# A decoder layer on one core: one grouped product in place of three in the compressed branch, and eight empty steps placed elsewhere

## The chip, the cores and the metric

The kernel runs on one core of a Trainium2 chip. The core has five engines with a queue each: TensorE (PE, and PEld for its weight loads), VectorE (DVE), ScalarE (ACT), GpSimd (POOL) and SyncE (SP, which issues most DMAs). The metric is device time in microseconds (us) of one execution. A measurement is the median of several runs, and one more execution is taken with the hardware profiler.

## The reference, cut to what matters

One layer of a decoder with 256 tokens of width 2048, all in float32. After an RMS norm and one input projection, two groups of heads run side by side: gated linear attention (GLA, 4 heads) and sparse attention (NSA, 8 query heads in 2 groups that share keys and values). Their outputs go into one output projection, then a SwiGLU feed-forward part (FFN) follows.

NSA has three branches: compressed, selected and sliding window. The compressed one is what the change touches:

```python
k_cmp = rms_norm(compress(heads(kc_raw, hk), k_pos, k_w1, k_w2), kc_g)
v_cmp = compress(heads(vc_raw, hk), v_pos, v_w1, v_w2)        # silu(flat @ w1) @ w2
...
sc = jnp.einsum('bhgqd,bhnd->bhgqn', qb, k_cmp) * scale
pc = jax.nn.softmax(jnp.where(mc, sc, NEG), axis=-1) * mc
o_cmp = jnp.einsum('bhgqn,bhnd->bhgqd', pc, v_cmp)
...
return gb[..., 0:1] * o_cmp + gb[..., 1:2] * o_sel + gb[..., 2:3] * o_win
```

There are only 15 compressed keys and values per head (`NCMP = 15`).

## The kernel before

**Three products for one.** The matrix products read float32 in a faster, less exact form (`F32R`). To keep the precision, a number is split into a high part, which is what that form can hold, and a low part, the rest. A product then becomes three: high times high, high times low, low times high. `split` (L131) does this for the weights: ACT writes `hi` (L137), DVE subtracts and writes `lo` (L138). `in_parts` (L637) does it for activations with ACT (L638) and DVE (L639). `chunk` (L273) issues the main stream of products (L283): 24 of 128x512 for every four tiles of 128 rows of weights, and each `hi`/`lo` pair of buffers serves 12 of them. Four such buffers of each exist.

**Main stream and side steps.** Most of the kernel before the FFN is written as generators. `drive` (L98) walks through the main generator (`proj` or `w_out_half`) and counts two units per product or pair of products; whenever the count reaches `pace`, `side` (L83) lets one side generator take one step, up to its next `yield`. `urgent` goes ahead of `later`. An empty step (a bare `yield`) takes the turn and issues nothing, so it lets the main stream run on by that much. The pace is 2.5 units (a step for each 1.25 products) while the projections of keys, values and queries run, and 2 (a step for each product) in `w_out_half(0)`, the first half of the output projection, which has 192 main products.

The generators in question, in their order in `later`:

- `gla_mix` (L644): `gla_decay(0)` makes the decay factors for two GLA heads on ACT and DVE, level by level (L542 to L564); after 4 empty steps `gla_scores` (L567) begins with its products (L581), which read them; `gla_out` (L599) follows one head behind.
- `compress` (L736): blocks of raw keys and values times `w1` (L766, weights by DMA from POOL's queue at L745), a SiLU (L778), then `w2` (L783 for keys, L799 for values). The values' result, 15 rows per head group, is split into `vcm[0]` (high) and `vcm[1]` (low). Both tiles have 128 rows and are zero below row 15.
- `nsa_mix` (L917): for each of four tiles (group kv, token half t) `nsa_scores` (L836), and one tile behind it `nsa_out` (L883). `nsa_scores` ends with the softmax of the compressed scores `c` (L863 to L874) and the scaling of the other probabilities (L880). In `nsa_out`, `turn(i)` transposes probabilities on PE (L210) and splits them; `turn(0)` is that of `c`. The products with the values (L913) then add up in one bank of PSUM: three for each `i`, with a step each.

`turn_q` (L825), an urgent one, waits 11 empty steps after a query projection, then transposes the queries (L210) that DVE has copied out of PSUM (L814). `sum_rows` (L1035) is a third kind: in the background it adds rows of FFN weights on DVE (L1046) and stores the sums by two DMAs from POOL's queue (L1050).

The framework that builds the program decides each engine's final order: text order is the priority, but an instruction that it expects to be ready late lets later ones pass. So the trace, not the text, tells where an instruction stands. Tiles named `g` come from pools of rotating buffers (`g4` 24, `g2` 13, `g1` 7).

Of the kernel before, what the change touches and what calls it, by code (L numbers as in the profile page):

```python
# [9 lines left out]
F32R = mybir.dt.float32r  # L10
BF16 = mybir.dt.bfloat16
AF = mybir.ActivationFunctionType
ALU = mybir.AluOpType
AX = mybir.AxisListType

P = 128
S = 256
# [9 lines left out]
NCMP = 15  # L27
# [10 lines left out]
def kernel(  # L38
# [4 lines left out]
    nc = tc.nc  # L43
    act, mm = nc.scalar.activation, nc.tensor.matmul
    TT, TS, STT = nc.vector.tensor_tensor, nc.vector.tensor_scalar, nc.vector.scalar_tensor_tensor
# [7 lines left out]
    cp = tc.alloc_tile_pool(name="cp", bufs=1)  # L53
# [5 lines left out]
    def slot(pool, tag, bufs, align=None):  # L59
        def f(shape, dt=F32):  # L60
            n_tiles[0] += 1
            return pool.tile([P] + list(shape), dt, tag=tag, bufs=bufs, name=f"{tag}_{n_tiles[0]}", align_bytes=align)
        return f
# [3 lines left out]
    g4, g2, g1, small = slot(gp, "g4", 24, LINE), slot(s2p, "g2", 13), slot(s1p, "g1", 7), slot(s1p, "sm", 12)  # L67

    def bank():
        n_tiles[0] += 1  # L70
        return pp.tile([P, 512], F32, tag="bank", name=f"bank_{n_tiles[0]}")
# [5 lines left out]
    def f32(t):  # L77
        return t.bitcast(F32)
# [94 lines left out]
    cw2 = cp.tile([P, 2, P], F32, name="cw2")  # L173
# [35 lines left out]
    def transpose(o, i, n=P):  # L209
        return nc.tensor.transpose(o, i, ident[:n, :n])  # L210
# [426 lines left out]
    def in_parts(hi, lo, ps):  # L637
        act(hi, ps, AF.Copy)  # L638
        last["d"] = TT(lo, ps, f32(hi), ALU.subtract)  # L639
# [4 lines left out]
    def gla_mix():  # L644
        res = [{} for _ in range(4)]
        yield from gla_decay(0)
        for _ in range(4):
            yield
        nxt = iter(())
        for h in range(4):  # L650
            if h == 1:
                nxt = gla_decay(1)
            if h == 2:
                yield from nxt
            for _ in gla_scores(h, res[h]):
                yield
                next(nxt, None)
            if h:
                yield from gla_out(h - 1, res[h - 1])
        for _ in range(7):  # L660
            yield
        yield from gla_out(3, res[3])


    st = {}
# [62 lines left out]

    kcm = cp.tile([P, 2 * NCMP], F32, name="kcm")

    vcm = [cp.tile([P, 2, P], F32R, name=f"vcm{i}") for i in range(2)]
    for v in vcm:
        nc.gpsimd.memset(f32(v), 0.0)
    N2 = 2 * NCMP

    def compress():  # L736

        uT = st["uT"]

        def rows_of(i):  # L740

            res = []
            for j in range(2):
                to, j0 = g4([8, P]), (i % 2 * 2 + j) * 1024
                nc.gpsimd.dma_start(to, (k_w1, v_w1)[i // 2][0, j0:j0 + 1024, :].rearrange("(j p) h -> p j h", p=P))  # L745
                res.append(to)
            return res

        nxt = rows_of(0)
        for w in range(2):  # L750
            ph = bank()
            nc.vector.memset(ph[:, :P], 0.0)
            for half in range(2):
                j0 = 16 * half
                r = nxt
                if 2 * w + half < 3:
                    nxt = rows_of(2 * w + half + 1)
                blk = g2([16, 2, NCMP])
                for h in range(2):
                    u = uT[:, w, h, j0:j0 + 240].rearrange("p (n j) -> p j n", j=16)  # L760
                    TT(blk[:, :, h, :], u, pos[:, w, j0:j0 + 16].unsqueeze(2).to_broadcast([P, 16, NCMP]), ALU.add)
                for _ in range(9):
                    yield
                for j in range(16):
                    g = 32 * (j % 4)
                    mm(ph[g:g + N2, :P], blk[:, j].rearrange("p h n -> p (h n)"), r[j // 8][:, j % 8, :], start=(half == 0 and j < 4),  # L766
                       stop=(half == 1 and j >= 12), tile_position=(0, g), skip_group_check=True)
                    if j % 16 == 15:
                        yield
            hs = g1([P])  # L770
            nc.vector.tensor_copy(hs, ph[:, :P])
            for _ in range(6):
                yield
            pt = bank()
            transpose(pt[:, :P], hs)
            hid = g1([32])
            nc.vector.tensor_reduce(hid, pt[:, :P].rearrange("p (g m) -> p m g", g=4), AX.X, ALU.add)
            act(hid, hid, AF.Silu)  # L778
            for _ in range(9):
                yield  # L780
            pk = bank()
            if w == 0:
                mm(pk[:N2, :P], hid[:, :N2], cw2[:, 0, :], start=True, stop=True)  # L783
                ss = small([1])
                junk = g1([P])
                act(junk[:N2], pk[:N2, :P], AF.Square, accum_out=ss[:N2])
                TS(ss[:N2], ss[:N2], 1.0 / 128, EPS, ALU.mult, ALU.add)
                rk = small([1])
                rsqrt_(rk[:N2], ss[:N2])
                kk = g1([P])  # L790
                TS(kk[:N2], pk[:N2, :P], rk[:N2], None, ALU.mult)
                for _ in range(25):
                    yield
                pt = bank()
                transpose(pt[:, :N2], kk[:N2, :], N2)
                TS(kcm, pt[:, :N2], kgain[:, 0:1], None, ALU.mult)
            else:
                for h in range(2):
                    mm(pk[:NCMP, h * P:(h + 1) * P], hid[:, h * NCMP:(h + 1) * NCMP], cw2[:, 1, :], start=True, stop=True)  # L799
                in_parts(vcm[0][:NCMP], vcm[1][:NCMP], pk[:NCMP, :S].rearrange("p (h d) -> p h d", h=2))  # L800
            yield

    nq, sc = {}, {}
# [19 lines left out]
        return f  # L823

    def turn_q(kv, q):  # L825
        for _ in range(11):
            yield
        qf, qh, ql = g4([4, S]), g4([4, S], F32R), g4([4, S], F32R)
        for pair in range(2):
            js = slice(2 * pair, 2 * pair + 2)  # L830
            ps = yield from turn_pair(q, pair)
            in_parts(qh[:, js], ql[:, js], ps)
            nc.scalar.copy(qf[:, js], ps)
        nq[kv] = qf, qh, ql

    def nsa_scores(kv, t, res):  # L836
# [5 lines left out]
        pr = [g4([2, 2, ns]) for _ in range(2)] if t else [g4([4, 2, ns])]  # L842
        pr = [pr[j // 2][:, j % 2] if t else pr[0][:, j] for j in range(4)]
        mxs, nb, sums = small([4, 2]), small([4, 2]), small([4, 2])
        pc_ = bank()
        for j in range(4):
            p = bank()
            sv = p[:, :2 * ns].rearrange("p (b s) -> p b s", b=2)
            for i, (a, b) in enumerate(((qh, kh), (qh, kl), (ql, kh))):
# [4 lines left out]
               start=True, stop=True)  # L854
# [7 lines left out]
        c = small([4, NCMP])  # L862
# [6 lines left out]
        sm = small([4])  # L869
# [1 line left out]
        nc.vector.reciprocal(sm, sm)  # L871
        TT(sm, sm, gv[:, 0, :], ALU.mult)
        TT(c, c, mone[:, t, :].unsqueeze(1).to_broadcast([P, 4, NCMP]), ALU.mult)
        TT(c, c, sm.unsqueeze(2).to_broadcast([P, 4, NCMP]), ALU.mult)  # L874
        rs = small([4, 2])
        nc.vector.reciprocal(rs, sums)
        TT(rs, rs, gv[:, 1:3, :].rearrange("p b h -> p h b"), ALU.mult)
        for j in range(4):
            for b in range(2):
                TS(pr[j][:, b, :], pr[j][:, b, :], rs[:, j, b:b + 1], None, ALU.mult)  # L880
        res.update(pr=pr, c=c)

    def nsa_out(kv, t, res):  # L883
        pr, c, tb = res["pr"], res["c"], slice(t * P, (t + 1) * P)
        if t == 0:
            m_h[2 + kv], m_l[2 + kv] = g4([4, S], F32R), g4([4, S], F32R)
        todo = [None] + [(b, s_) for b in range(2) for s_ in range(t + 1)]
        pts = []

        def turn(i):  # L890
            pt = bank()
            n = P if i else NCMP
            parts = [g2([512], F32R) for _ in range(2)]
            if i == 0:
                for a in parts:
                    nc.gpsimd.memset(f32(a), 0.0)
            for j in range(4):
                src = pr[j][:, todo[i][0], todo[i][1] * P:(todo[i][1] + 1) * P] if i else c[:, j, :]
                transpose(pt[:n, j * P:(j + 1) * P], src)
                if j % 2:  # L900
                    yield
            pts.append(parts)
            in_parts(parts[0][:n], parts[1][:n], pt[:n, :])

        po = bank()
        yield from turn(0)
        yield from turn(1)
        for i, at in enumerate(todo):
            if i + 2 < len(todo):
                yield from turn(i + 2)  # L910
            vh, vl = (st[v][:, at[0], at[1], kv * P:(kv + 1) * P] for v in ("vh", "vl")) if i else (v[:, kv, :] for v in vcm)
            for j, (v, p) in enumerate(((vh, pts[i][0]), (vh, pts[i][1]), (vl, pts[i][0]))):
                mm(po, v, p, start=(i == 0 and j == 0), stop=(i == len(todo) - 1 and j == 2))  # L913
                yield
        put_mix(2 + kv, slice(0, 4), tb, po.rearrange("p (j s) -> p j s", j=4))

# [460 lines left out]
```

## Time and profile before

| what | value |
|---|---|
| time, median of 3 runs | 1110.05 us (1109.75 to 1110.84) |
| time of the profiled execution | 1109.58 us |
| its span, first to last instruction | 1107.9 us |
| TensorE clock granted | 1.000 throughout |
| bytes moved | 259.61 MB, mean 234 GB/s |

The profiled execution is 1.7 us longer than its span, which is what lies around the instructions. A profile lists busy time per engine, a picture of the span in 40 slices of 27.7 us, the chain of work that ended last, and groups of instructions. Further views show single instructions in order of time (start in us, duration in us, engine, line, what it writes and reads, shapes, count; in brackets the idle time of the engine and what ended it), windows of time with the busy time of each engine, and who waited for whom. A busy PE is not a PE at its peak, because products overlap: what one costs in a stream is the distance from start to start. In time, the span goes: loading and the first projections to about 84 us, projections with GLA beside them to about 260, NSA beside the last projection and the first half of the output projection to about 370, the second half to about 418, the FFN to the end.

### The profile page before, as it was taken

To read this page: it belongs to the slowest core of one execution; us is meant where nothing else is said; L and a number is where in the kernel's file an instruction comes from. 1 tells how busy PE (TensorE), PEld (TensorE's weight loads), DVE (VectorE), ACT (ScalarE), POOL (GpSimd) and SP (SyncE) were. 2 spreads that over 40 slices of the span, in tenths; PEclk is the share of its full clock that TensorE was granted. 3 is DMA by queue.
4 is the path that set the end of the run, shared out by engine and by line. 5 is a ranking of instruction groups with operands and counts; after the bars stand their busy time and mean duration, and the time that the engine had idled before them with its cause. 6 is when DMAs were issued, how large, how long until landed. Compare 5 with 4: busy or idle time off the path is not lost.

```text
span 1107.9 us, 14624 instructions
## 1 busy us (share of the span) xinstructions
PE 1097.7 (99%) x5298; PEld 900.7 (81%) x5298; DVE 991.5 (89%) x1277; ACT 741.5 (67%) x1009; POOL 74.0 (7%) x139
## 2 busy tenths in 40 slices
PE   9999999999999999999999999999999999999998
PEld 8888887897777887888888888888888888887886
DVE  6678779987589788997999999999999999999997
ACT  7645557555566586667586866768586866767684
POOL 4110000123101000000000000000000000000000
PEclk9999999999999999999999999999999999999999
DMA  7999985568846656785565657576566657476663
GB/s 272 336 337 361 368 285 187 188 227 286 282 183 225 218 185 215 244 305 202 192 223 198 217 197 251 187 248 212 206 228 213 213 197 255 167 267 220 234 229 114
DMA packets 124850, 259.61 MB, mean 234 GB/s; under 512 B 6709, under 2 KB 8793, under 8 KB 124778
## 3 DMA queue, kind: packets, MB, share of 16 engines
q1 hardware_dynamic: 113514, 219.86, 57.3%
q0 software_dynamic: 10368, 37.75, 9.2%
q10 hardware_dynamic: 896, 1.07, 0.3%
q8 instruction: 41, 0.67, 0.2%
q14 instruction: 31, 0.25, 0.1%
HBM read 239.78 MB, written 18.87 MB: 233 GB/s over the span
## 4 chain that ended last, share of the span: by engine, by line
PE 83%; DVE 6%; DMA 6%; issue 2%; ACT 2%; SPq 0%; POOL 0%; ACTq 0%; POOLq 0%; DVEq 0%
PE bank L283 39%; PE bank L1114 35%; DMA raw<-in_w_in_dram 3%; PE bank L210 3%; DMA g<-in_w_up_dram 2%; PE bank L1255 2%; DVE ftwo L639 2%; DVE lo L138 2%; PE bank L913 1%; PE bank L850 1%; ACT hi L137 1%; PE bank L581 1%; DMA fraw<-in_w_down_dram 1%; DVE g L1145 0%; DVE g L1046 0%
## 5 line engine op out<-in xcount | busy, mean ns | idle before, releaser
L1114 PE MATMUL bank<-ftwo,g 128*128 128x512 f32 x1848 | 431.6, 392 | 0.2 <-ACT ftwo L638 0.2
L1114 PEld LDWEIGHTS bank<-ftwo,g 128*128 128x128 f32 x1848 | 342.4, 188 | 76.6 <-DVE ftwo L639 3.5
L283 PE MATMUL bank<-hi,g 128*128 128x512 f32 (+1 forms) x1088 | 321.7, 375 | 1.3 <-ACT hi L323 1.3
L639 DVE TENSOR_TENSOR ftwo<-fraw,ftwo 128x1536 fp32r<-128x1536 f32 (+1 forms) x130 | 257.6, 1982 | 9.0 <-ACT ftwo L638 7.6
L638 ACT ACTIVATE ftwo<-fraw 128x1536 fp32r<-128x1536 f32 (+1 forms) x130 | 217.0, 1671 | 32.7 <-DMA fraw<-in_w_up_dram 13.8
L283 PE MATMUL bank<-ftwo,g 128*128 128x512 f32 x960 | 221.4, 391 | 1.0 <-ACT bank L1226 1.0
L283 PEld LDWEIGHTS bank<-hi,g 128*128 128x128 f32 x1088 | 192.4, 188 | 31.4 <-ACT hi L323 1.7
L283 PEld LDWEIGHTS bank<-ftwo,g 128*128 128x128 f32 x960 | 179.2, 188 | 40.5 <-ACT bank L1226 3.1
L283 PE MATMUL bank<-lo,g 128*128 128x512 f32 (+3 forms) x544 | 194.5, 377 | 0.0
L137 ACT ACTIVATE hi<-raw 128x1024 fp32r<-128x1024 f32 (+3 forms) x124 | 130.7, 1057 | 90.5 <-PE bank L283 74.3
L138 DVE TENSOR_TENSOR lo<-raw,hi 128x1024 fp32r<-128x1024 f32 (+3 forms) x124 | 150.1, 1217 | 38.0 <-ACT hi L137 37.3
L638 ACT ACTIVATE ftwo<-g 128x1024 fp32r<-128x1024 f32 x74 | 78.2, 1057 | 69.0 <-DVE g L1145 43.7
L283 PEld LDWEIGHTS bank<-lo,g 128*128 128x128 f32 x544 | 98.6, 189 | 15.9 <-issue 0.8
L639 DVE TENSOR_TENSOR ftwo<-g,ftwo 128x1024 fp32r<-128x1024 f32 x74 | 90.2, 1219 | 10.7 <-ACT ftwo L638 10.7
L639 DVE TENSOR_TENSOR ftwo<-fsum,ftwo 128x1024 fp32r<-128x1024 f32 x74 | 90.1, 1217 | 0.0
L638 ACT ACTIVATE ftwo<-fsum 128x1024 fp32r<-128x1024 f32 x74 | 77.5, 1048 | 8.6 <-DVE fsum L1147 7.4
L1238 ACT COPY g<-bank 128x512 f32<-128x512 f32 x80 | 45.9, 589 | 39.7 <-PE bank L283 37.8
L1145 DVE TENSOR_TENSOR g<-fraw 128x1024 f32<-128x1024 f32 x56 | 67.4, 1217 | 0.0
L1226 ACT COPY bank<-g 128x512 f32<-128x512 f32 x80 | 45.2, 592 | 13.1 <-DVE f L1175 11.5
L638 ACT ACTIVATE g<-bank 128x512 fp32r<-128x512 f32 (+1 forms) x50 | 29.2, 592 | 36.2 <-PE bank L210 29.0
L1103 POOL DMA_DIRECT2D g<-sums x16 | 8.5, 533 | 512.1 <-DVE ftwo L639 482.3
L210 PE MATMUL bank<-ident,g 128*128 128x128 f32 (+2 forms) x214 | 40.1, 278 | 1.2 <-DVE g L814 0.5
(241 smaller groups left out, 902.2 us busy)
## 6 DMA issues: line engine op xcount, KB each, us to landing
fraw<-in_w_gate_dram SPq DMA_DIRECT2D x86, 512.0 KB, 3.8
fraw<-in_w_down_dram SPq DMA_DIRECT2D x42, 1024.0 KB, 5.0
raw<-in_w_in_dram SPq DMA_DIRECT2D x36, 1024.0 KB, 7.5
fraw<-in_w_up_dram SPq DMA_DIRECT2D x70, 512.0 KB, 4.6
sums<-g POOLq DMA_DIRECT2D x32, 512.0 KB, 6.5
raw<-in_w_out_dram SPq DMA_DIRECT2D x16, 1024.0 KB, 5.3
g<-in_w_gate_dram SPq DMA_DIRECT2D x16, 512.0 KB, 8.4
g<-in_w_up_dram SPq DMA_DIRECT2D x16, 512.0 KB, 8.6
```

Source lines behind the costliest of these rows:

```text
L137: act(h[:, i:i + n], r[:, k + i:k + i + n], AF.Copy)
L138: last["d"] = TT(o[:, i:i + n], r[:, k + i:k + i + n], f32(h[:, i:i + n]), ALU.subtract)
L210: return nc.tensor.transpose(o, i, ident[:n, :n])
L283: last["mm"] = mm(bk[t], a[:, k, t * P:(t + 1) * P], m[:, off:off + w], start=(first_ and k == 0 and i == 0), stop=(end and k == 3 and i = ...
L581: mm(p[:, j * P:(j + 1) * P], u, w, start=True, stop=True)
L638: act(hi, ps, AF.Copy)
L639: last["d"] = TT(lo, ps, f32(hi), ALU.subtract)
L1114: mm(banks[q], x, m, start=todo[q] == total[q], stop=todo[q] == 1)
L1145: TT(s1, r[:, 1:3], r[:, 3:4].to_broadcast([P, 2, 512]), ALU.add)
L1226: nc.scalar.copy(banks[qs[n][t]], h_sb[n][:, t, :])
L1238: nc.scalar.copy(h_sb[n][:, t, :], bs[t])
L1255: mm(bk, u, m, start=(first and i == 0), stop=(end and i == 2), skip_group_check=onto)
```

## The change

Three groups of 15 rows, each starting at a multiple of 32 (rows 0, 32 and 64, 79 rows in all), hold probabilities high, low, high and values high, high, low. One product over these rows adds up what three products gave.

```diff
     def gla_mix():
         yield from gla_decay(0)
-        for _ in range(4):
+        for _ in range(9):
             yield
...
-    vcm = [cp.tile([P, 2, P], F32R, name=f"vcm{i}") for i in range(2)]
-    for v in vcm:
-        nc.gpsimd.memset(f32(v), 0.0)
+    vcm = cp.tile([P, 2, P], F32R, name="vcm")
+    G3, N3 = 32, 2 * 32 + NCMP
+    def thrice(a):
+        return a.unsqueeze(2).to_broadcast([P, a.shape[1], 3, NCMP])
+    def groups(a):
+        return a[:, :, :3 * G3].rearrange("p h (g n) -> p h g n", n=G3)[:, :, :, :NCMP]
...
-            act(hid, hid, AF.Silu)
+            if w == 0:
+                act(hid, hid, AF.Silu)
+            else:
+                hid3 = g2([2, P])
+                nc.gpsimd.memset(hid3, 0.0)
+                act(groups(hid3), thrice(hid[:, :N2].rearrange("p (h n) -> p h n", h=2)), AF.Silu)
...
-                    mm(pk[:NCMP, h * P:(h + 1) * P], hid[:, h * NCMP:(h + 1) * NCMP], cw2[:, 1, :], start=True, stop=True)
-                in_parts(vcm[0][:NCMP], vcm[1][:NCMP], pk[:NCMP, :S].rearrange("p (h d) -> p h d", h=2))
+                    mm(pk[:N3, h * P:(h + 1) * P], hid3[:, h, :N3], cw2[:, 1, :], start=True, stop=True)
+                pv = pk[:, :S].rearrange("p (h d) -> p h d", h=2)
+                act(vcm[:N3], pv[:N3], AF.Copy)
+                at = slice(2 * G3, N3)
+                TT(vcm[at], pv[at], f32(vcm[at]), ALU.subtract)
...
     def turn_q(kv, q):
-        for _ in range(11):
+        for _ in range(14):
             yield
...
-        TT(c, c, sm.unsqueeze(2).to_broadcast([P, 4, NCMP]), ALU.mult)
+        c3 = g2([4, P])
+        nc.gpsimd.memset(c3, 0.0)
+        TT(groups(c3), thrice(c), sm.unsqueeze(2).unsqueeze(3).to_broadcast([P, 4, 3, NCMP]), ALU.mult)
...
-            n = P if i else NCMP
-            parts = [g2([512], F32R) for _ in range(2)]
-            if i == 0:
-                for a in parts:
-                    nc.gpsimd.memset(f32(a), 0.0)
+            n = P if i else N3
+            parts = [g2([512], F32R) for _ in range(2 if i else 1)]
...
-            in_parts(parts[0][:n], parts[1][:n], pt[:n, :])
+            if i:
+                in_parts(*parts, pt)
+            else:
+                mid, at = parts[0], slice(G3, G3 + NCMP)
+                act(mid[:N3], pt[:N3], AF.Copy)
+                TT(mid[at], pt[at], f32(mid[at]), ALU.subtract)
...
+            if i == 0:
+                mm(po, vcm[:N3, kv, :], pts[0][0][:N3], start=True, stop=False)
+                yield
+                continue
```

`nsa_scores` hands on `c3` in place of `c`, and `turn(0)` transposes 79 columns of it per head, where it transposed 15.

More of the change, by code (lines that the diff above doesn't have):

```diff
@@ L880, in nsa_scores @@
                 TS(pr[j][:, b, :], pr[j][:, b, :], rs[:, j, b:b + 1], None, ALU.mult)
-        res.update(pr=pr, c=c)
+        res.update(pr=pr, c=c3)
     def nsa_out(kv, t, res):
@@ L891, in turn @@
             pt = bank()
-            n = P if i else NCMP
-            parts = [g2([512], F32R) for _ in range(2)]
-            if i == 0:
-                for a in parts:
-                    nc.gpsimd.memset(f32(a), 0.0)
+            n = P if i else N3
+            parts = [g2([512], F32R) for _ in range(2 if i else 1)]
             for j in range(4):
-                src = pr[j][:, todo[i][0], todo[i][1] * P:(todo[i][1] + 1) * P] if i else c[:, j, :]
+                src = pr[j][:, todo[i][0], todo[i][1] * P:(todo[i][1] + 1) * P] if i else c[:, j, :N3]
                 transpose(pt[:n, j * P:(j + 1) * P], src)
@@ L910, in nsa_out @@
                 yield from turn(i + 2)
-            vh, vl = (st[v][:, at[0], at[1], kv * P:(kv + 1) * P] for v in ("vh", "vl")) if i else (v[:, kv, :] for v in vcm)
+            if i == 0:
+                mm(po, vcm[:N3, kv, :], pts[0][0][:N3], start=True, stop=False)
+                yield
+                continue
+            vh, vl = (st[v][:, at[0], at[1], kv * P:(kv + 1) * P] for v in ("vh", "vl"))
             for j, (v, p) in enumerate(((vh, pts[i][0]), (vh, pts[i][1]), (vl, pts[i][0]))):
-                mm(po, v, p, start=(i == 0 and j == 0), stop=(i == len(todo) - 1 and j == 2))
+                mm(po, v, p, start=False, stop=(i == len(todo) - 1 and j == 2))
                 yield
```

## The prediction

> **What bounds the kernel now.** First the page: busy time of the engines, the picture in slices, and the chain that ended last. In the first row each engine has its busy time, share and count.
>
> ```profile
> PE 1097.7 (99%) x5298; PEld 900.7 (81%) x5298; DVE 991.5 (89%) x1277; ACT 741.5 (67%) x1009; POOL 74.0 (7%) x139
> ...
> DVE  6678779987589788997999999999999999999997
> ...
> PE 83%; DVE 6%; DMA 6%; issue 2%; ACT 2%; SPq 0%; POOL 0%; ACTq 0%; POOLq 0%; DVEq 0%
> ```
>
> PE carries 83% of the chain, and DVE is close behind it in many slices. So a product taken from PE counts in full only where DVE isn't late. The busy time by windows shows where that is (window, its length, then busy us and instructions of PE, PEld, DVE, ACT, POOL, the clock, DMA share, GB/s); the second row of the fence is the stage where GLA's first scores are made, the last two are NSA's.
>
> ```profile
> 171.05:193.45 22.40, 21.11 (x114) 17.20 (x113) 20.88 (x65) 17.08 (x40) 1.36 (x2) 1.00 0.50 168
> 193.45:205.30 11.85, 11.85 (x57) 9.31 (x56) 11.85 (x28) 7.54 (x14) 0.00 (x0) 1.00 0.48 154
> ...
> 304.00:340.00 36.00, 36.00 (x202) 28.66 (x202) 31.41 (x103) 25.41 (x69) 1.55 (x3) 1.00 0.48 173
> 340.00:372.00 32.00, 32.00 (x163) 25.40 (x162) 27.99 (x57) 16.55 (x35) 3.60 (x7) 1.00 0.65 223
> ```
>
> From 304 to 372 PE never stands and DVE has 8.6 us to spare (4.59 and 4.01): PE bounds the stage that loses the products. From 171 to 205 DVE has 1.52 us to spare in 34: both bound it, and what PE gains there can be lost again.
>
> **The products.** The view of the tile `vcm` and the order in time on PE:
>
> ```profile
> L913 PE MATMUL bank<-g,vcm x12: 388/394/426, 323.1 to 362.6; 128*128 128x512 f32 x12
> ```
> ```profile
> 339.78 1.55 PE L913 MATMUL bank<-g,g 128*128 128x512 f32 x6
> ```
>
> Twelve products with `vcm`, three for each of four tiles, become four: eight go. One lasts 394 ns alone, but six in a row take 1.55 us, so the distance is (1.55 - 0.39) / 5 = 0.232 us. Eight are **1.86 us**. The new ones stream the same 512 columns over 79 rows in place of 128; no row of the trace has 79 rows. Bounds: no cheaper than nothing (2.8 us saved: twelve times 0.232), no dearer than two old ones each (0.93 saved); I take the old price, since L913's row is of the same shape but for the zero rows. [...]
>
> The other PE work changes in size, not in number: 16 transposes of `c` write 79 rows for 15, and `w2`'s two products load 79 columns.
>
> ```profile
> 358.44 0.38 PE L210 MATMUL bank<-ident,sm 128*15 128x128 f32 x2
> 358.58 0.48 PE L283 MATMUL bank<-hi,g 128*128 128x512 f32 x1
> ...
> 363.04 0.38 PE L210 MATMUL bank<-ident,g 128*128 128x128 f32 x2
> 363.18 0.48 PE L283 MATMUL bank<-hi,g 128*128 128x512 f32 x1
> ```
>
> A pair of 15 columns (`sm`) and one of 128 (`g`) both let the next product start 0.14 us later, and 79 lies between: 0.
>
> **The copies.** ACT's copy of `c` and DVE's subtraction keep their columns, 512; DVE's subtraction also keeps its 15 rows, now from row 32.
>
> ```profile
> L874 DVE TENSOR_TENSOR sm<-sm,sm 128x60 f32<-128x60 f32 x4 | 0.8, 206 | 0.0
> ...
> L639 DVE TENSOR_TENSOR g<-bank,g 15x512 fp32r<-15x512 f32 x4 | 2.7, 676 | 1.3 <-ACT g L638 1.3
> ```
>
> L874 writes 180 elements in place of 60. Between its 0.206 us and the 0.42 of a 128x256 one (L555, below) that is some 0.34 us, four times 0.13 more. The SiLU grows likewise, once. This lies on DVE and ACT in the stage with 8.6 us to spare: 0 on PE; if that cover were gone, 0.5 us.
>
> ```profile
> 345.19 0.67 DVE L1046 TENSOR_TENSOR g<-g 128x512 f32<-128x512 f32 x1
> 345.79 0.67 DVE L856 TENSOR_REDUCE sm<-bank 128x2 f32<-128x512 f32 x1
> ```
>
> DVE starts an instruction 0.07 us before the one ahead ends. [...]
>
> The single product now needs ACT's copy and DVE's subtraction, where the first of three needed the copy only: 0.68 us more delay. Behind it on PE wait the other products of the same bank; the main stream goes on meanwhile, one product per step: 0.
>
> **The first scores.** Around the first products of `gla_scores`:
>
> ```profile
> 175.40 0.39 PE L283 MATMUL bank<-hi,g 128*128 128x512 f32 x1
> 177.08 0.49 PE L581 MATMUL bank<-g 128*128 128x128 f32 x2 [1.29 <-DVE g L555]
> ...
> 183.51 0.47 PE L283 MATMUL bank<-hi,g 128*128 128x512 f32 x1
> 183.82 0.38 PE L581 MATMUL bank<-g,g 128*128 128x128 f32 x2
> ```
> ```profile
> 176.61 0.42 DVE L555 TENSOR_TENSOR g<-g,g 128x256 f32<-128x256 f32 x1
> ```
>
> From L283 to L581 it is 1.68 us, undisturbed 0.31: PE stands 1.37 us for a level that DVE finishes at 177.03. Five steps at pace 2.5 put 6.25 main products ahead.
>
> ```profile
> 564.40 21.92 PE bank L283 x96
> ```
>
> A main product costs 21.92 / 96 = 0.228 us in a stream (chain of waits), so PE gets 1.43 us of other work: the wait is covered, **1.37 us**.
>
> Is it kept? That is the doubtful step. DVE's work up to the next weights doesn't shrink:
>
> ```profile
> 192.26 0.17 DVE L615 TENSOR_SCALAR sm<-sm 128x2 f32<-128x2 f32 x1 [0.50 <-ACT g L613]
> ...
> 193.45 1.22 DVE L138 TENSOR_TENSOR lo<-raw,hi 128x1024 fp32r<-128x1024 f32 x1
> ```
> ```profile
> 181.28 1.06 ACT L137 ACTIVATE hi<-raw 128x1024 fp32r<-128x1024 f32 x1 [0.29 <-PE bank L283]
> ```
> ```profile
> 194.72 0.50 PE L283 MATMUL bank<-lo,g 128*128 128x512 f32 x1
> ```
>
> This `lo` is done at 194.67 and read at 194.72: no slack. Its `hi` was there from 182.34, so it stood in DVE's order behind GLA work, the last of which (L615) waited for score products. With PE 1.37 us ahead it is needed at 193.35. But the scores come five steps later against the main stream, so what hangs on them (L615, the last masks) should fall behind this L138 in the order, which brings it forward by the 1.2 us or more needed. I take the gain as kept; the other end, nothing kept, is the first rival.
>
> **The queries.** The transposes of `turn_q`:
>
> ```profile
> 266.35 0.27 PE L210 MATMUL bank<-ident,g 128*128 128x128 f32 x1
> 267.14 0.33 PE L210 MATMUL bank<-ident,g 128*128 128x128 f32 x1 [0.51 <-DVE g L814]
> ```
> ```profile
> 266.39 0.69 DVE L814 COPY g<-bank 128x512 f32<-128x512 f32 x1
> ```
>
> Two transposes stand 0.11 us apart undisturbed (0.38 - 0.27 in the x2 rows above), here 0.79: PE waits **0.68 us** for the second copy. Three steps are 3.75 products, 0.86 us: covered. What is late next is nothing near: DVE's copies end at 267.08.
>
> **What is moved.** What follows in `later` shifts against the main stream: 5 steps later, 3 more behind each `turn_q`, and two earlier again with each of the four tiles, 3 later in the end. `compress` thus issues its weight DMAs (L745, POOL's queue, past the stores of L1050) up to 6 main products later and uses them up to 11 later, so they land with more room. The last `nsa_out` step then comes 3 main products later:
>
> ```profile
> 0.00:370.05 370.05, 335.67 (x1437) 243.69 (x1438) 1.00 0.77 269
> ```
>
> This counts L283 alone: the last L913 stands behind main product 1438, and `w_out_half(0)` ends with 1440 (192 in the first projection, 480 in the next five, 96 + 96 + 192 + 96 + 96, 192). So the last step just fits or is left over alone. Left over, it costs one wait for a copy, from 0 to 0.7 us (L639's 0.68); the second half of the projection begins with products that don't need it, so I take 0.
>
> **Sum.** 1.86 + 1.37 + 0.68 = 3.91 us, say 3.9. The profiled execution has 1109.58 us and a span of 1107.9; it becomes 1105.7, span 1104.0. The median of the runs, 1110.05, is 0.47 above that execution, so the median should be **1106.1 us**. About 0.2% (2.2 us) is what a measurement can tell from no change; the forecast is 0.36%.
>
> **Rivals.**
>
> *DVE takes the first gain back.* DVE's order stays, `lo` is done at 194.67 as before, and PE stands there for what it didn't at 175. For: 1.52 us of spare time in 34. Against: the order goes by the text, and the text moves the scores. Gain 1.86 + 0.68 = 2.5: 1107.5.
>
> *Only the products count.* The new order makes waits like the two removed elsewhere, as two waits of 1.37 and 0.68 us came about before. Gain 1.86: 1108.2.
>
> *The zeros come late.* `c3` is cleared by POOL ahead of DVE's L874; before, the clearing stood ahead of ACT's copy. POOL's queue stands still where it holds a store that waits for DVE:
>
> ```profile
> 309.24 1.01 POOL L896 MEMSET g<- 128x512 f32 x2
> 340.89 0.53 POOL L1050 DMA_DIRECT2D sums<-g  x1 [30.64 <-PE bank L913]
> ```
> ```profile
> 324.76 0.21 DVE L874 TENSOR_TENSOR sm<-sm,sm 128x60 f32<-128x60 f32 x1
> ...
> 333.42 1.22 DVE L138 TENSOR_TENSOR lo<-raw,hi 128x1024 fp32r<-128x1024 f32 x1
> ```
> ```profile
> 338.31 0.48 PE L283 MATMUL bank<-lo,g 128*128 128x512 f32 x1
> ```
>
> If the clearing of the second tile's `c3` lands behind that store, it ends at 340.89 + 0.53 + 0.5 = 341.9, and DVE stands from 324.76, 17.2 us, with the `lo` of 333.42 behind it. PE reads that `lo` at 338.31, 3.7 us after its end, so 17.2 - 3.7 = 13.5 us are lost: 1106.1 + 13.5 = 1119.6, slower. It decides once the clearing ends after 324.76 + 3.7 = 328.5. Against: POOL has little to do, and ran the old clearings (309.24) long ahead of their use.
>
> **How the numbers follow.** Forecast 0.48, DVE takes it back 0.22, only the products 0.20, late zeros 0.05, other new waits that eat all 0.05. The forecast is faster by over 0.2%; 1107.5 stands just inside that bound (1107.8), so of its 0.22 I count 0.14 as faster and 0.08 as the same; only the products is the same; of the last, 0.03 is the same and 0.02 slower. Faster 0.62, same 0.31, slower 0.07. The range goes up to 1109.6, the third case with 0.7 for the step left over and 0.7 for the last tile's single product if it waits for both copies uncovered; down to 1104.4, the forecast with 0.9 for products that cost nothing and 0.8 for the two waits of PEld for `lo` (total, times, longest in the view of waits), should they go; the late zeros stay out.
>
> ```profile
> PEld bank L283 <- DVE lo L138: 0.8, 2, 0.4
> ```
>
> **What would show it.** Four products with `vcm` at the old distance (0.23). No idle time at L581's first products nor at L210 after L814. The `lo` used near 193.4 done before; if PE stands there for L138, the first rival is right. The clearing of `c3` on POOL done long before L874. If the span falls by less than 1.5 us, the price of the 79 rows or the cover of the stage was wrong.

## The result, and the profile after

| | before | changed |
|---|---|---|
| median of 6 runs | 1110.01 us (1109.53 to 1110.84) | 1115.97 us (1114.52 to 1120.70) |
| profiled execution | 1109.58 us | 1115.84 us |
| its span | 1107.9 us | 1114.1 us |

The change makes the kernel slower: the ratio is 1.0060, with a 95% interval of 1.0041 to 1.0078. The forecast was 1106.1 us.

The busy row of the changed kernel's page:

```profile
PE 1098.8 (99%) x5290; PEld 901.4 (81%) x5290; DVE 992.8 (89%) x1277; ACT 741.4 (67%) x1009; POOL 72.1 (6%) x134
```

Eight products are gone from the count (5298 before, 5290 now), yet PE is busy for 1.1 us more (1097.7 before): some of its instructions have become slower. The loss arises ahead of the FFN, whose first product on PE starts 7.4 us later (the first row is of the kernel before, the second of the changed one):

```profile
417.69 0.39 PE L1114 MATMUL bank<-hi,g 128*128 128x512 f32 x1
425.14 0.39 PE L1137 MATMUL bank<-hi,g 128*128 128x512 f32 x1
```

The FFN itself is then 1.2 us shorter. The waits of PE say where PE stood. The columns are what waited, on what, us in total, times, longest. Before:

```profile
PE bank L283 <- ACT hi L323: 1.3, 1, 1.3
PE bank L581 <- DVE g L555: 1.3, 1, 1.3
...
PE bank L283 <- ACT bank L1226: 1.0, 1, 1.0
PE bank L210 <- DVE g L814: 0.5, 1, 0.5
PE bank L210 <- DVE g L714: 0.3, 1, 0.3
```

The changed kernel:

```profile
PE bank L773 <- DMA g<-in_cmp_v_w_dram: 3.2, 2, 2.1
PE bank L210 <- DVE g L829: 2.1, 2, 1.3
PE bank L931 <- DVE g L922: 1.7, 1, 1.7
PE bank L283 <- ACT hi L323: 1.5, 1, 1.5
...
PE bank L210 <- DVE g L714: 0.7, 1, 0.7
PE bank L283 <- DVE lo L138: 0.4, 1, 0.4
```

The wait at the first scores (L581, 1.3) is gone, as meant. The wait in the query turn (L814, now L829) went from 0.5 to 2.1. Two larger waits are new: `compress` waits 3.2 us for the weights of the values (L773, before L766), and the grouped product waits 1.7 us for DVE (L931). The wait at L1226 lies in the FFN, whose code the change doesn't touch. Still, the profiles of the three kernels here with three products have it (1.0, 0.4 and 0.9 us), and none of the nine with the grouped product has more than 0.2 us there; why is not shown.

The largest wait, that for the weights, in order of time on PE (start, duration, instruction, and in brackets the wait):

```profile
302.77 0.64 PE L773 MATMUL bank<-g,g 128*30 128x128 f32 x16 [1.13 <-DMA g<-in_cmp_v_w_dram]
...
305.48 1.08 PE L773 MATMUL bank<-g,g 128*30 128x128 f32 x16 [2.06 <-DMA g<-in_cmp_v_w_dram]
```

The same sixteen products last 0.64 us the first time and 1.08 the second. The windows of PE around them show what differs (window, length, PE's busy us and count, granted clock, DMA share, GB/s):

```profile
304.00:306.00 2.00, 0.53 (x12) 0.63 0.91 324
306.00:308.00 2.00, 2.00 (x16) 0.50 1.04 419
308.00:310.00 2.00, 2.00 (x7) 0.50 0.70 283
310.00:311.00 1.00, 1.00 (x4) 0.50 0.02 8
311.00:313.00 2.00, 2.00 (x10) 0.92 0.00 0
```

Behind the wait the granted clock is 0.50 for some 5 us, and the main products there start 0.43 us apart (308.78 and 309.21 on PE), where it was 0.228 in the stream of before. So, as an estimate, busy time by what the clock lacks is lost: 0.53 x 0.37 + 5.00 x 0.50 + 2.00 x 0.08 = 2.9 us.

This adds up to the difference of the spans. The waits that grew or are new bring 3.2 + (2.1 - 0.5) + 1.7 + (0.7 - 0.3) + 0.4 + (1.5 - 1.3) = 7.5 us, those that went take 1.3 + 1.0 = 2.3, the low clock brings 2.9, the eight products take 1.9: 7.5 - 2.3 + 2.9 - 1.9 = 6.2, and the spans differ by 1114.1 - 1107.9 = 6.2.

Why do the weights come late? POOL's queue in order of time, before:

```profile
270.65 2.71 POOL L745 DMA_DIRECT2D g<-in_cmp_v_w_dram  x3 [0.26 <-PE bank L766]
274.38 0.88 POOL L745 DMA_DIRECT2D g<-in_cmp_v_w_dram  x1 [1.01 <-DVE g L761]
...
292.80 2.57 POOL L213 TENSOR_TENSOR sc<-sc,mhalf 128x8 f32<-128x8 f32 x1 [10.28 <-DVE sc L818]
```

and in the changed kernel:

```profile
256.18 1.77 POOL L752 DMA_DIRECT2D g<-in_cmp_k_w_dram  x2 [7.39 <-DMA sums<-g]
257.96 0.72 POOL L213 TENSOR_TENSOR sm<-sm,mhalf 128x2 f32<-128x2 f32 x1
...
264.32 1.01 POOL L890 MEMSET g<- 128x512 f32 x2
...
272.61 1.83 POOL L752 DMA_DIRECT2D g<-in_cmp_v_w_dram  x2
...
293.13 2.57 POOL L213 TENSOR_TENSOR sc<-sc,mhalf 128x8 f32<-128x8 f32 x1 [8.26 <-DVE sc L833]
295.65 1.82 POOL L752 DMA_DIRECT2D g<-in_cmp_v_w_dram  x2
```

Before, all four loads for the values were issued by 275.3, and then POOL stood in front of the rsqrt of the second query block (L213 of `ev_nq(1)`, 292.80), which must wait for the projection. In the changed kernel two of the four stand *behind* that rsqrt and are issued at 295.65, 21 us later; PE stands for the first of them from 301.64 on (302.77 less 1.13). Two of the clearings of `c3` (L890) ran at 264, far ahead of their use (L891, at 323 and 333).

### The profile page after: what moved, and what is told of

Same layout as the page of the kernel before. It is cut to its first block, busy times and chain, and to the rows that moved or that the text cites. A ratio compares the mean times of both kernels' runs of the same rounds, so it can differ in the third digit from the quotient of the medians.

```text
span 1114.1 us, 14602 instructions
## 1 busy us (share of the span) xinstructions
PE 1098.8 (99%) x5290; PEld 901.4 (81%) x5290; DVE 992.8 (89%) x1277; ACT 741.4 (67%) x1009; POOL 72.1 (6%) x134
## 4 chain that ended last, share of the span: by engine, by line
PE 83%; DMA 6%; issue 4%; DVE 3%; ACT 2%; POOL 1%; SPq 0%; ACTq 0%; POOLq 0%; DVEq 0%
PE bank L1137 39%; PE bank L283 36%; DMA raw<-in_w_in_dram 3%; PE bank L210 3%; DMA g<-in_w_up_dram 2%; PE bank L1278 2%; DVE lo L138 1%; DMA g<-in_cmp_v_w_dram 1%; PE bank L936 1%; PE bank L865 1%; ACT hi L137 1%; PE bank L581 1%; DMA sums<-g 1%; DVE g L1069 1%; POOL sm L213 0%
## 5 line engine op out<-in xcount | busy, mean ns | idle before, releaser
L639 DVE TENSOR_TENSOR ftwo<-fraw,ftwo 128x1536 fp32r<-128x1536 f32 (+1 forms) x130 | 257.6, 1982 | 7.9 <-ACT ftwo L638 6.5
L138 DVE TENSOR_TENSOR lo<-raw,hi 128x1024 fp32r<-128x1024 f32 (+3 forms) x124 | 150.1, 1217 | 34.7 <-ACT hi L137 33.5
L639 DVE TENSOR_TENSOR ftwo<-g,ftwo 128x1024 fp32r<-128x1024 f32 x74 | 90.2, 1218 | 10.6 <-ACT ftwo L638 10.6
L639 DVE TENSOR_TENSOR ftwo<-fsum,ftwo 128x1024 fp32r<-128x1024 f32 x74 | 90.1, 1217 | 0.0
L638 ACT ACTIVATE g<-bank 128x512 fp32r<-128x512 f32 x46 | 27.3, 596 | 38.0 <-PE bank L210 30.6
L210 PE MATMUL bank<-ident,g 128*128 128x128 f32 (+3 forms) x230 | 42.2, 276 | 3.2 <-DVE g L829 2.1
L210 PEld LDWEIGHTS bank<-ident,g 128*128 128x128 f32 (+3 forms) x230 | 30.0, 141 | 15.6 <-issue 3.1
```

Source lines behind the costliest of these rows:

```text
L138: last["d"] = TT(o[:, i:i + n], r[:, k + i:k + i + n], f32(h[:, i:i + n]), ALU.subtract)
```

## The experiments

**Theory A, the queue:** the added steps push the issue of the last two loads past `ev_nq(1)`, so they fall behind its rsqrt in POOL's order; the wait and the low clock behind it are most of the loss. **Theory B, the grouping:** the single product, which needs both ACT and DVE, and the instructions at rows 32 and 64 cost more than the eight products save. In the changed kernel that product waits 1.74 us once (L931), and the first subtraction at row 32 (L922) starts 0.04 us after the instruction in front ends, where one at row 0 started 0.08 us ahead of that end before (336.43).

**1. Products only.** The changed kernel with the old numbers of steps:

```diff
-        for _ in range(9):     # gla_mix
+        for _ in range(4):
-        for _ in range(14):    # turn_q
+        for _ in range(11):
```

> The changed kernel with the old numbers of steps (4 ahead of the first scores, 11 in the query turn): only the grouping of the products is left. Theory A, the queue: the loss is a place on POOL's queue, where the last two loads of the values' weights come behind the rsqrt of the second query block (L213). Here the start of the values' half falls 9 main products earlier, so they stand ahead of it, the 3.5 us of L773 behind them and the low clock after it are gone, and what is left is the saving of eight products: 1108.2 us (1107.0 to 1109.5). [...]

Measured: 1108.13 us against 1109.70 for before on the same chip, ratio 0.9986 (0.9977 to 0.9995). The grouping alone makes the kernel faster. Theory B falls.

**2. Steps only.** The kernel before with 9 and 14 steps:

> The kernel before with the new numbers of steps (9 and 14), three products as before. Theory A: the loads stand behind L213 here too, so PE waits some 3.5 us in L773's place at about 302 us and runs some 2 us at a low clock after it; with the gain of the scores' wait and without that of the products 1115 to 1118 us. Theory B: the steps take away 1.4 and 0.7 us of waits and nothing else happens: 1108 to 1109.

Measured: 1119.48 us, ratio 1.0084 (1.0067 to 1.0100). The loss comes with the steps alone, even a little more than theory A gave. Its waits of PE and its clock show the same two things, in a kernel with three products for each tile:

```profile
PE bank L766 <- DMA g<-in_cmp_v_w_dram: 3.5, 2, 2.3
```
```profile
306.00:308.00 2.00, 2.00 (x6) 0.56 0.83 333
```

**3. Nine and eleven.** The changed kernel with 11 steps in the query turn:

> The changed kernel with 11 steps in the query turn in place of 14, but 9 ahead of the first scores. Theory A: the start of the values' half falls at about main product 1245, three ahead of the second query block's at 1248, so all four loads stand ahead of L213: no wait at L773 above 0.3 us, no low clock around 306 us, some 5.5 to 7 us less than the changed kernel: 1109 to 1111. Theory B: three steps of a turn cannot matter to the products: within 1.5 us of the changed kernel, 1114.5 to 1117.

Measured: 1109.66 us, ratio 1.0001 (0.9992 to 1.0010). Three steps fewer, and the wait at L773 is gone: the loads are ahead of the rsqrt again. So the edge lies between five added steps and eight, at 1.25 main products each between 6 and 10 products. But the five steps gain nothing over run 1, which was 1.5 us faster. The waits of PE and the clock say what they cost:

```profile
PE bank L210 <- DVE g L829: 2.9, 2, 2.1
```
```profile
268.00:271.00 3.00, 2.57 (x12) 0.72 0.23 93
271.00:275.00 4.00, 4.00 (x43) 0.79 0.76 270
```

The transposes of the queries wait 2.9 us for DVE's copies, and by the same estimate 2.57 x 0.28 + 4.00 x 0.21 = 1.6 us go to the clock behind that.

**4. Early loads.** All eight steps kept, only the two loads issued five empty steps earlier, which puts them ahead of the rsqrt:

```diff
-                if 2 * w + half < 3:
+                if 2 * w + half < 2:
                     nxt = rows_of(2 * w + half + 1)
+                elif half == 0:
+                    nxt = nxt3
...
-                for _ in range(25):
+                for _ in range(20):
+                    yield
+                nxt3 = rows_of(3)
+                for _ in range(5):
                     yield
```

> The changed kernel with all its steps, but with the last two loads of the values' weights issued five steps earlier, so that they stand ahead of L213 on POOL's queue; every other step stays in its place. Theory A: the wait at L773 (3.2 us) and the low clock after it (some 2.4 us) go and nothing else does: 1110 to 1111.5, and the waits at 265 to 268 us (2.1 us, query turn) and at 331 us (1.7 us, L931) stay. Theory B, the grouping or the steps themselves: at most 1 us less, 1115 to 1116.5. If the low clock comes from something else than the wait, the wait alone goes: 1112 to 1113.

Measured: 1111.11 us, ratio 1.0011 (1.0002 to 1.0020). One place on a queue is worth 1.0060 - 1.0011 = 0.49%, 5.4 us by the ratios and 1115.97 - 1111.11 = 4.9 by the medians, of a loss of 6.7 and 6.0. Its waits of PE keep the two others:

```profile
PE bank L936 <- DVE g L927: 1.8, 1, 1.8
PE bank L210 <- DVE g L834: 1.5, 2, 0.8
```

and a low clock has come up behind the first of them (PE stands from 325.15 to 326.90):

```profile
324.00:328.00 4.00, 2.25 (x11) 0.96 0.80 257
328.00:330.00 2.00, 2.00 (x7) 0.50 0.03 10
330.00:333.00 3.00, 3.00 (x15) 0.81 0.00 0
```

By the same estimate that is 2.25 x 0.04 + 2.00 x 0.50 + 3.00 x 0.19 = 1.7 us. So run 4 took away 3.2 us of waiting at L773, 2.9 of low clock behind it and 0.6 in the query turn, and lost 1.7 here: 5.0 us, where the spans differ by 1114.1 - 1109.4 = 4.7. The waits at the start of the kernel (L323, L324) differ from run to run and are left out of this.

**5. Three query steps.** The changed kernel with 4 steps ahead of the first scores and 14 in the query turn:

> The changed kernel with 4 steps ahead of the first scores, as before, and its 14 in the query turn. The loads of the values' weights stand ahead of L213 of the second query block. If the three steps do what they are for: against the run with the products only (1108.1 us, with 1.0 us of wait at 266 us) that wait goes and nothing comes: 1107.1 (1106.5 to 1107.8). Rival: they move the second query block's scores as well, and the single product at L931 then waits for DVE's subtraction as in the changed kernel (1.9 us, and a low clock after it in one run): 1109 to 1110.5.

Measured: 1107.87 us against 1110.45, ratio 0.9971 (0.9961 to 0.9982). That lies between the time of the theory (1107.1) and that of the rival. Against run 1's ratio of 0.9986 a gain is likely, but the intervals overlap. In its profile the wait in the query turn is gone and none has come at L931, so the rival falls; but a new one stands at 261 us, where PE waits 1.1 us for GLA's last head (L622 on DVE, behind L617, for which DVE stood 2.58 us until POOL's rsqrt was done; the next run has more of that).

**6. The rsqrt ahead.** In the changed kernel POOL stood 7.39 us for a store to land (POOL's rows above, 256.18) before it could issue two loads for the keys, and the rsqrt of GLA's last head stood behind them. DVE waited for it:

```profile
258.72 0.17 DVE L617 TENSOR_SCALAR sm<-sm 128x2 f32<-128x2 f32 x1 [3.52 <-POOL sm L213]
```

Run 4 with these two loads behind that rsqrt:

```diff
-        nxt = rows_of(0)
+        nxt, ahead = rows_of(0), last["rs"]     # the latest rsqrt
...
-                    nxt = rows_of(2 * w + half + 1)
+                    with behind(ahead if 2 * w + half == 0 else None):
+                        nxt = rows_of(2 * w + half + 1)
```

> The run with the early loads (1111.1 us), and besides the second half of the keys' weights is issued behind the rsqrt of GLA's last head (L213 at 257.8 us) in place of ahead of it. Theory: in that run POOL stood 6.5 us in front of these loads, the rsqrt behind them came 2.6 us late to DVE, and DVE's copies of the queries with it; so the wait in the query turn (1.8 us in two parts at 266 to 268 us) should go to at most 0.4: 1109.3 to 1110. Rival: DVE is late at 266 because it has too much to do with five steps less of time, and the stand only used up slack: 1110.7 to 1111.5, with the wait where it was.

Measured: 1108.40 us, ratio 0.9978 (0.9969 to 0.9987); run 4 had 1.0011. DVE's row now:

```profile
256.69 0.17 DVE L617 TENSOR_SCALAR sm<-sm 128x2 f32<-128x2 f32 x1 [0.84 <-POOL sm L213]
```

The stand fell from 2.59 us in run 4 to 0.84, and no wait for L834 is left among PE's waits. The rival (DVE simply has too much to do) falls. By the spans (1109.4 and 1106.8) the gain is 2.6 us, more than the wait's 1.5; this execution has no low clock behind its grouped product either, though the wait there is the same (L937, 1.8 us):

```profile
328.00:330.00 2.00, 2.00 (x10) 1.00 0.00 0
```

**7. The grouped product as the fourth.** DVE's rows in the changed kernel in front of the first grouped product, and PE's row:

```profile
329.83 1.22 DVE L138 TENSOR_TENSOR lo<-raw,hi 128x1024 fp32r<-128x1024 f32 x1
...
332.22 0.16 DVE L894 TENSOR_TENSOR sm<-sm,gate 128x8 f32<-128x8 f32 x1
332.42 0.68 DVE L922 TENSOR_TENSOR g<-bank,g 15x512 fp32r<-15x512 f32 x1
333.13 0.35 DVE L891 TENSOR_TENSOR g<-sm,sm 128x180 f32<-128x180 f32 x1
```
```profile
333.15 0.51 PE L931 MATMUL bank<-g,vcm 79*128 79x512 f32 x1 [1.74 <-DVE g L922]
```

The subtraction (L922) stands behind this L138, another of 1.22 us ahead of it (328.57), a 128x512 one of 0.68 us and a row of small ones, and PE starts the product as soon as it is done. Run 4 with the product behind the three of the first pair, which need the copies of another tile:

```diff
             if i == 0:
-                mm(po, vcm[:N3, kv, :], pts[0][0][:N3], start=True, stop=False)
-                yield
                 continue
...
-                mm(po, v, p, start=False, stop=(i == len(todo) - 1 and j == 2))
+                mm(po, v, p, start=(i == 1 and j == 0), stop=(i == len(todo) - 1 and j == 2))
                 yield
+            if i == 1:
+                mm(po, vcm[:N3, kv, :], pts[0][0][:N3], start=False, stop=False)
+                yield
```

> The run with the early loads (1111.1 us), and besides the grouped product is the fourth in each accumulation, behind the three products of the first pair, in place of the first; it computes the same. Theory: the first of three products needed ACT's copy only, the single one needs DVE's subtraction as well, and that stands behind two L138 and ten small instructions of DVE; three products later it is done. So the 1.9 us at L936 and the low clock behind it (some 1.4 us more from 328 to 332 us) go: 1107.8 to 1109.3. Rival: the first product of the next pair is as late, since DVE writes its low part behind the same row: the wait moves there and the time stays within 0.7 us, 1110.4 to 1111.8.

Measured: 1110.10 us (12 runs, 1107.18 to 1112.55), ratio 0.9994 (0.9985 to 1.0004), 1.9 us less than run 4 by the ratios, though the intervals overlap. That lies between the two, and PE's order of time says so too:

```profile
329.19 0.50 PE L939 MATMUL bank<-g,g 128*128 128x512 f32 x1 [1.08 <-ACT g L638]
```

The wait did move to the next pair, as the rival had it, but it waits for ACT's copy there and is 1.1 us for 1.8. The profiled execution is one of the longest three of the twelve (1111.57 us), and its span, 1109.8, is no shorter than run 4's. It has a wait for the queries of 2.1 us in two parts, as the changed kernel has, and here a low clock follows it:

```profile
270.00:272.00 2.00, 2.00 (x9) 0.63 0.06 23
272.00:274.00 2.00, 2.00 (x7) 0.51 0.76 225
```

By the same estimate that is 2.00 x 0.37 + 2.00 x 0.49 = 1.7 us, ahead of the place that this edit touches.

**8. All three.** Runs 4, 6 and 7 together:

> The changed kernel with the early loads, the rsqrt ahead of the keys' loads, and the grouped product as the fourth. If the three faults are all there is and add up, the gains of the prediction come out but for what DVE takes back at 193 and 212 us (1.0 us): 1106.3 to 1107.5. If one of them only hid another, 1108 or more.

Measured: 1106.51 us against 1110.45, ratio 0.9961 (0.9949 to 0.9973). It is faster than both kernels. Its longest wait of PE behind the start of the kernel, and the first product of its FFN:

```profile
PE bank L940 <- ACT g L638: 1.1, 1, 1.1
```
```profile
415.42 0.39 PE L1144 MATMUL bank<-hi,g 128*128 128x512 f32 x1
```

No wait for weights and none for the queries is left, and the clock stayed at 1. By the ratios it gains 1.9 us over run 6, as run 7 did over run 4, again with intervals that overlap. Its span is 3.4 us shorter than that of the kernel before (1104.5 for 1107.9): 2.3 us of this lie ahead of the FFN (415.42 for 417.69) and 1.1 in the FFN.

**9 and 10. What the parts are worth there.** Run 8 with the old numbers of steps (and without the earlier issue of the two loads, which stand ahead of the rsqrt there anyway), and the kernel before with the added steps and the two moves on POOL's queue (runs 4 and 6), so with three products for each tile:

> The run with all three repairs, but with the steps of before (4 and 11); the loads of the values' weights need no help then. It tells what the added steps are worth once nothing is in their way. By the two waits that they cover (1.45 us at 175 us; 1.0 us in the query turn of the run with the products only) less the 1.0 us that DVE takes back at 193 and 212 us it should be 1.4 us slower than all three: 1107.9 (1107.2 to 1108.6). If the repairs alone did it, the same as all three within 0.4 us.

> The kernel before with the new numbers of steps (9 and 14), the early loads and the rsqrt ahead of the keys' loads, but with three products with vcm for each tile. It tells what the grouping is worth there. By eight products at 0.232 us it is 1.9 us slower than all three: 1108.4 (1107.6 to 1109.2), and about as fast as the same with the grouped product first (1108.4), whose wait at L937 gives that saving back. If the first of three products has to wait as long, 1109.5 or more.

Measured: 1108.41 us against 1110.22, ratio 0.9985 (0.9976 to 0.9994), and 1109.18 us, ratio 0.9990 (0.9981 to 0.9998). Run 9 is as fast as run 1 (0.9986), so the moves of runs 6 and 7 alone, without the steps, gain nothing. Run 10 against run 2 (1.0084) shows the two moves on POOL's queue once more, in a kernel without the grouped product: 0.94%, some 10 us. With nothing in their way the added steps are worth 0.9985 - 0.9961 = 0.24%, 2.7 us, and the grouping, as the fourth product, 0.29%, 3.2 us; the intervals are wide enough (some 2 us to either side) to hold the forecast's terms, 2.05 for the steps and 1.86 for the products.

The profiles say where the grouping's part lies. Run 10's FFN begins at

```profile
416.34 0.39 PE L1120 MATMUL bank<-hi,g 128*128 128x512 f32 x1
```

which is 0.9 us later than in run 8, and its span (1107.4) is 2.9 us longer. So 2.0 of the 2.9 us lie in the FFN, where the forecast has no term. The FFN takes 690.2 to 691.0 us, from its first product to the end of the span, in the three profiles with three products and 688.9 to 689.6 in the nine with the grouped one. Whether the grouping does this, and how, stays open.

## Why the prediction was wrong, point by point

**The step that failed** is in "What is moved": `compress` "issues its weight DMAs (L745, POOL's queue, past the stores of L1050) up to 6 main products later and uses them up to 11 later, so they land with more room". It looked at the stores on POOL's queue and not at the rsqrts. The shift of the use is right in size: PE has started 1265 main products when the first product with the values' weights begins in the kernel before, and 1276 in the changed one. That of the issue isn't, for the last two loads: they stand nine empty steps ahead of these products in both kernels, so they move by the same ten or eleven products and not by 6. Run 3, with 1270, shows that a shift of about that size would have left them ahead of the rsqrt. Above all it is no shift in time: on POOL the loads passed from the front of an instruction that it waits for (until 292.80 before, 293.13 in the changed kernel) to behind it, where they were issued at 295.65. They came 21 us later for a shift of ten products, some 2.3 us at 0.228 each. Run 4 undoes this place alone and wins back 4.9 us of 6.0 by the medians, 5.4 of 6.7 by the ratios.

**The query turn.** The step "What is late next is nothing near: DVE's copies end at 267.08" held DVE's times of before for fixed. In the changed kernel the second copy ends at 268.64 (its row starts at 267.97 and has 0.67): the wait grew from 0.5 to 2.1 us where 0.68 should have gone. Run 6 shows the cause, again on POOL's queue: two loads that wait for a store, and an rsqrt for DVE behind them. With that mended the wait goes.

**The grouped product.** The step "the main stream goes on meanwhile, one product per step: 0" was wrong. The 0.68 us of later start were right as DVE's own part, but DVE's part starts behind two L138 of 1.22 us each, and PE started no other product in the 1.74 us for which this one waited (333.15 above): it held up the main stream behind it. That cost 1.7 us once, in the first tile; before, the first of three products had only needed ACT's copy. Run 7 shows that 0.7 of the 1.8 us in run 4 lay in this place; 1.1 moves to the next pair, where PE waits for ACT's copy.

**The first scores.** The wait of 1.37 us went, but DVE took part of it back: a new wait of 0.4 us for L138 and one of 0.7 for 0.3 at L714. The first rival ("DVE takes the first gain back") was half right. The step "brings it forward by the 1.2 us or more needed" was right in size: the subtraction came forward by 1.34 us (193.45 before, 192.11 now), though still behind L615, as these rows of the changed kernel's DVE and PE show. What failed is the time at which it is needed: PE came to it 1.71 us earlier than before (194.72, now 193.39 less 0.38), not 1.37, and was there first.

```profile
192.04 0.16 DVE L615 TENSOR_SCALAR sm<-sm 128x2 f32<-128x2 f32 x1
192.11 1.22 DVE L138 TENSOR_TENSOR lo<-raw,hi 128x1024 fp32r<-128x1024 f32 x1
```
```profile
193.39 0.50 PE L283 MATMUL bank<-lo,g 128*128 128x512 f32 x1 [0.38 <-DVE lo L138]
```

**The products.** 1.86 us was right in kind; its size is not shown. Run 1 gains 0.14% (0.05 to 0.23), 1.6 us, but by its profile only 1.0 of that lies ahead of the FFN (its first product starts at 416.71, before at 417.69), and run 10 against run 8 has 0.9 there. The price of 79 rows was right: in run 8 the next product starts 0.23 us behind such a one, the old distance.

```profile
328.59 0.40 PE L943 MATMUL bank<-g,vcm 79*128 79x512 f32 x1
328.82 0.86 PE L940 MATMUL bank<-g,g 128*128 128x512 f32 x3
```

So eight products less should give PE 1.86 us, and other waits take a part of it back, such as the 1.1 us at L940.

**The copies.** The product of 180 elements (L891) takes 0.35 us, where 0.34 was estimated. The subtraction at row 32 costs DVE some more: L922 starts at 332.42, 0.04 us after L894 ends, and L891 starts 0.03 us after L922 ends, where before the subtraction of the second tile (L639, at 336.43) started 0.08 us ahead of the end of the instruction in front, and the next one 0.07 us ahead of its end. That is 0.2 us, which three of the four L922 show; the other waits 0.19 us for ACT's copy and has only the second part. Why they start later is not shown: L639 on 128 rows also starts 0.04 us after an L894 ends (346.06 in the changed kernel). The estimate for all five subtractions is 1.0 us of DVE at most, and run 1, which has them all, is faster all the same.

**The rivals.** "Only the products count" gave 1108.2, and run 1 has 1108.13, but for another reason: there the steps are not in it. That is luck. "The zeros come late" had the right queue and the wrong instruction: the last clearing (L890) does stand behind a store, until 342.50, but L891 needs it at 366.28 only. What came true, loads behind a waiting rsqrt, was among none of them. The sum itself, 1106.1, is near what the change gives once three places are mended (run 8: 1106.51), but in part by luck: of run 8's 3.4 us of span only 2.3 lie ahead of the FFN, where all of the forecast's 3.9 should lie.

## What to carry to other kernels

When steps are added ahead of a load, list every instruction on the queue that issues it, with what each waits for; ask not how much later the load comes but what it now stands behind. A queue that holds both small arithmetic for other engines and long transfers can turn a shift of some 2 us into a delay of 21, as here, and one waiting transfer delays the arithmetic behind it in turn (here loads that POOL stood 7.39 us for, and DVE 3.52 us for the rsqrt behind them). When several products become one, the one needs every operand at the start: look for a place where all are done, not where the first was (here that took away 0.7 of 1.8 us of waiting).

## What the hardware showed beside this

The granted clock fell to 0.50 behind PE's wait at L773 in the changed kernel, and that cost nearly as much as the standing: 2.9 us, by the estimate above, behind 3.2 us of waiting. The length of the wait alone doesn't decide it at around 2 us: 1.8 us at L936 in run 4 brought 1.7 us of low clock, 1.8 us at L937 in run 6 none; and 2.1 us in two parts for the queries brought none in the changed kernel and 1.7 in run 7. What else decides it is not shown. After the waits that add up to more within a few microseconds it fell each time: 2.9 us in run 3, 3.5 in run 2, 3.2 in the changed kernel. The longest single wait among these was 2.3 us (L766 in run 2).
